# Retention of a hybrid decoder step: sample states by products of 32 rows, the head norm by ones on all partitions, and gate steps among the last head's chunks

## The chip, the cores and the metric

The kernel runs on one core of a Trainium2 chip. A core has engines with queues of their own: TensorE (PE, and PEld for loading its weights), VectorE (DVE), ScalarE (ACT), GpSimd (POOL) and SyncE (SP), which starts most transfers. The metric is the time of one execution on the device in microseconds (us); smaller is better.

## The reference

One inference step of one layer: FFN, a mixer of two branches (stick-breaking attention and retention), and another FFN. It takes a prompt of 1024 tokens and 8 decode samples of 8 tokens each. The change lies in retention (4 heads, 128 wide keys, 256 wide values) and the norm behind it:

```python
def step(S, inp):
    qi, ki, vi = inp
    inner = jnp.einsum('bhcd,bhsd->bhcs', qi, ki) * decay_in[None]
    o = jnp.einsum('bhcs,bhsv->bhcv', inner, vi) + jnp.einsum('bhcd,bhdv->bhcv', qi, S) * decay_q
    S = S * decay_c + jnp.einsum('bhsd,bhsv->bhdv', ki * decay_k, vi)
    return S, o
...
o_r, new_state = retention(q_r, k_r, v_r, ret_state)
o_rf = o_r.astype(F32)
o_rf = o_rf * lax.rsqrt(jnp.mean(o_rf * o_rf, axis=-1, keepdims=True) + NORM_EPS)
o_r = (o_rf.reshape(B, T, RET_V_WIDTH) * ret_gn_g.astype(F32)).astype(u.dtype)
o_r = jax.nn.silu(g_r) * o_r
m = jax.nn.sigmoid(a_sb) * (o_sb @ w_sb_out) + jax.nn.sigmoid(a_r) * (o_r @ w_ret_out)
```

The prompt starts from a zero state; each sample starts from its own state of 128 x 256 per head (`state_ret`), gives 8 rows of output from it and hands a new state back.

## The kernel before

Activations lie with channels on the partitions and the 1088 tokens (1024 of the prompt, 64 of the samples) along the columns. Products are in float32 precision by two means. `mm3` splits both factors into a high and a low half (`hi` on ACT, `lo` on DVE, lines 96 and 99; type fp32r) and multiplies three times (lines 133, 137, 138). A few products take plain f32 operands; the trace shows each of those as two records of MATMUL where an fp32r product is one.

`mixer_in` runs, after some of the gates: `retention()` over four heads; then 40 fill steps (`FILL_RET`); then the prompt's stick-breaking attention, 12 fill steps (`FILL_SB`) and the samples' attention over the cached pages (decode, line 1115). A fill step is three matmuls (one mm3 of one of the 8 blocks of K) of a gate projection (`gate_steps`) or of the output projection of retention (`ret_steps`); the last of a tile passes through a `gs` tile on its way to DRAM. Fill steps are also interleaved with both attentions until their supply ends, so their total is fixed. `mixer_out` follows, and begins with loads of `osT` that need the decode's last output (`odec`).

For each head, `retention()` projects q, k, v and two gates (bank `pa`), turns q and k by rope, transposes v (`ev_v`), and then goes over the prompt in four chunks of 256 tokens. A chunk makes the scores (bank `pb`), masks them (`rsc`), multiplies by v and by the state (`po`), calls `finish`, updates the state (bank `pm`), and calls `sample_states` for two of the eight samples. After the four chunks `finish` is called once more for the 64 sample tokens. So there are 16 calls of `sample_states`, and 20 of `finish`.

`sample_states` multiplies, for each sample, the 64 x 256 values under a mask (`km` x `vdn`, line 1371: the mask keeps the sample's 8 rows, a DVE operation at line 1370 and a POOL memset) and the sample's masked queries by its old state (`qm` x `s0`, line 1366, into `po_s`), and adds on DVE (line 1373). `finish` evicts the output (`oc`), squares it on ACT (439), adds (441), sums the partitions by products with one column of ones (464), forms 1/root for rows (478 on DVE, a power on POOL), makes diagonal matrices (489), and spreads them over the partitions by another product with ones (496), before DVE scales (1315) and gates (1318).

The order of instructions on each engine is set by a scheduler that simulates a timeline when the program is built; the code's order and the buffers bound it. `fill(k, after)` pins its steps behind the instruction `after`. On the chip each engine runs its list in order.

## Time and profile before

| | us |
|---|---|
| three runs | 2891.10, 2893.32, 2895.43 |
| median | 2893.32 |
| the profiled execution | 2891.72 |
| its span in the trace | 2889.2 |
| PE busy | 2798.6 (97%) |
| DVE busy | 2017.1 (70%) |
| ACT busy | 1245.3 (43%) |
| POOL busy | 738.5 (26%) |

The span is the time from the first to the last instruction that the trace holds. Times in the trace count from the span's start. Retention lies between about 820 and 1276 us, the prompt's attention behind it, decode ends at about 1940 us, and `mixer_out` begins there. PE's matmuls overlap: the time that one costs is the distance from its start to the start of the next, not its own duration. PE's granted clock is 0.99 of full speed in the mean.

### The profile page before, as it was taken

Reading aid. Unit: us, or ns where it says so; the run is one execution under the profiler, and the core shown is the slowest. Engines: PE = TensorE matmul, PEld = TensorE weight load, DVE = VectorE, ACT = ScalarE, POOL = GpSimd, SP = SyncE. Lnnn points to the kernel's source line nnn. Section 1 sums busy time; section 2 is a strip of 40 time slices with the busy share of each in tenths; the row PEclk is TensorE's granted clock in tenths of the full one; section 3 lists DMA queues with packets and bytes.
Section 4 is the critical chain, followed back from the end, with each engine's and each line's share of the span. In section 5 each row is a group of like instructions: output and inputs, shape, how many; then the busy total and the mean of one; then the engine's idle time right before and its main releaser. Section 6 shows DMA issues by size and latency. Waiting matters only on the chain.

```text
span 2889.2 us, 51617 instructions
## 1 busy us (share of the span) xinstructions
PE 2798.6 (97%) x20064; PEld 2633.3 (91%) x20064; DVE 2017.1 (70%) x3922; ACT 1245.3 (43%) x2546; POOL 738.5 (26%) x679
## 2 busy tenths in 40 slices
PE   7999999999999999999999889989999999999998
PEld 7898899999999999989999867768989988999997
DVE  7888878888753553546888744436578888688776
ACT  6444444444343333335666543213354444544443
POOL 0234513333150000000000245520013334233321
PEclk9999999999999999999999999999999999999999
DMA  6444444333252322333222389876333336333431
GB/s 177 145 127 144 140 155 123 110 112 108 80 162 83 99 84 86 94 113 80 76 74 76 123 294 332 297 244 198 105 96 121 119 110 189 122 103 107 130 89 42
DMA packets 420420, 380.63 MB, mean 132 GB/s; under 512 B 30352, under 2 KB 380944, under 8 KB 420176
## 3 DMA queue, kind: packets, MB, share of 16 engines
q1 hardware_dynamic: 397904, 306.03, 34.6%
q0 software_dynamic: 22272, 71.31, 7.4%
q8 instruction: 157, 2.57, 0.4%
q14 instruction: 87, 0.71, 0.1%
HBM read 310.03 MB, written 63.05 MB: 129 GB/s over the span
## 4 chain that ended last, share of the span: by engine, by line
PE 59%; DVE 5%; DMA 3%; issue 2%; POOL 1%; ACT 1%; SPq 0%; DVEq 0%; POOLq 0%; ACTq 0%
PE pa L133 10%; PE pa L138 10%; PE pa L137 10%; PE pb L133 3%; PE pb L138 3%; PE pb L137 3%; PE pc L137 3%; PE pc L138 3%; PE pc L133 3%; PE pc L1202 2%; PE pm L1011 1%; PE pm L1115 1%; PE pc L999 1%; DVE sl L99 1%; DMA ul<-orT 1%
## 5 line engine op out<-in xcount | busy, mean ns | idle before, releaser
L96 ACT ACTIVATE sh<-wr 128x512 fp32r<-128x512 f32 x592 | 340.0, 624 | 364.1 <-POOL wr L590 135.5
L133 PE MATMUL pa<-uh,wh 128*128 128x384 f32 (+1 forms) x1408 | 476.7, 339 | 4.2 <-ACT qdec L920 2.0
L138 PE MATMUL pa<-uh,wl 128*128 128x384 f32 (+1 forms) x1408 | 464.4, 330 | 0.0
L137 PE MATMUL pa<-ul,wh 128*128 128x384 f32 (+1 forms) x1408 | 463.5, 329 | 0.4 <-POOL ul L99 0.4
L99 DVE TENSOR_TENSOR sl<-wr,sh 128x512 fp32r<-128x512 f32 x592 | 398.8, 701 | 60.2 <-ACT sh L96 56.8
L133 PE MATMUL pa<-q,sh 128*128 128x256 f32 (+1 forms) x1408 | 410.4, 292 | 15.7 <-DVE p L648 7.8
L137 PE MATMUL pa<-q,sh 128*128 128x256 f32 (+1 forms) x1408 | 409.5, 291 | 2.2 <-DVE q L99 2.2
L138 PE MATMUL pa<-q,sl 128*128 128x256 f32 (+1 forms) x1408 | 408.5, 290 | 0.3 <-DVE sl L99 0.3
L137 PE MATMUL pc<-hl,whd 128*128 128x256 f32 (+2 forms) x1088 | 350.4, 324 | 2.6 <-DVE hl L99 2.6
L138 PE MATMUL pc<-hh,wld 128*128 128x256 f32 (+2 forms) x1088 | 350.0, 323 | 0.0
L133 PE MATMUL pc<-hh,whd 128*128 128x256 f32 (+2 forms) x1088 | 343.6, 324 | 4.5 <-DVE y L718 2.5
L718 DVE TENSOR_TENSOR y<-y,pc 128x256 f32<-128x256 f32 (+2 forms) x496 | 250.1, 516 | 135.8 <-PE pc L138 133.9
L133 PE MATMUL pb<-q,sh 128*128 128x288 f32 (+1 forms) x1088 | 314.8, 290 | 6.5 <-ACT sh L96 4.9
L138 PE MATMUL pb<-q,sl 128*128 128x288 f32 (+1 forms) x1088 | 314.6, 289 | 0.5 <-DVE sl L99 0.4
L137 PE MATMUL pb<-q,sh 128*128 128x288 f32 (+1 forms) x1088 | 314.9, 290 | 0.0
L133 PEld LDWEIGHTS pa<-q,sh 128*128 128x128 f32 x1408 | 268.2, 191 | 20.8 <-DVE p L648 8.8
L133 PEld LDWEIGHTS pa<-uh,wh 128*128 128x128 f32 x1408 | 265.7, 189 | 20.1 <-issue 10.0
L137 PEld LDWEIGHTS pa<-q,sh 128*128 128x128 f32 x1408 | 268.0, 190 | 4.7 <-DVE q L99 2.7
L137 PEld LDWEIGHTS pa<-ul,wh 128*128 128x128 f32 x1408 | 265.7, 189 | 3.3 <-issue 1.4
L138 PEld LDWEIGHTS pa<-q,sl 128*128 128x128 f32 x1408 | 267.2, 190 | 1.5 <-DVE sl L99 0.5
L138 PEld LDWEIGHTS pa<-uh,wl 128*128 128x128 f32 x1408 | 265.2, 188 | 2.7 <-issue 1.7
L588 POOL TENSOR_TENSOR wr<-wr 128x512 f32<-128x512 f32 x76 | 108.2, 1424 | 495.5 <-DVE sl L99 495.4
(340 smaller groups left out, 5958.3 us busy)
## 6 DMA issues: line engine op xcount, KB each, us to landing
wr<-in_w_ffn_gu_dram SPq DMA_DIRECT2D x176, 512.0 KB
wrd<-in_w_ffn_down_dram SPq DMA_DIRECT2D x88, 512.0 KB
wr<-in_w_in_dram SPq DMA_DIRECT2D x56, 512.0 KB
q<-cB SPq DMA_DIRECT2D x16, 576.0 KB
wr<-in_w_o_dram SPq DMA_DIRECT2D x10, 512.0 KB
cB<-y SPq DMA_DIRECT2D x32, 144.0 KB
cB<-xr SPq DMA_DIRECT2D x32, 144.0 KB
s<-in_state_ret_dram SPq DMA_DIRECT2D x16, 256.0 KB
```

The lines of the kernel that those rows point to most:

```text
L96: return self.nc.scalar.activation(dst, src, AF.Copy)
L99: (eng or self.nc.vector).tensor_tensor(dst, src, hi.bitcast(F32), op=ALU.subtract)
L133: ins = mm(ps, wh, xh, start=first, stop=False)
L137: mm(ps, wh, xl, start=False, stop=False)
L138: mm(ps, wl, xh, start=False, stop=last)
L588: tt(v1, v0, v1, op=ALU.add)
L718: nc.vector.tensor_tensor(y[p][:, d, c], y[p][:, d, c], ps[:, :n], op=ALU.add)
L999: nc.tensor.transpose(tp[:, j * P : (j + 1) * P], bt[:, j * P : (j + 1) * P], self.ident)
L1011: ins = nc.tensor.matmul(po[:, lo:256], vs[:, j, :], ats[j // 4][x][:, j % 4, lo:256], start=(j == 0 and x == 0), stop=(j == last and x == 1))
L1115: return nc.tensor.matmul(out[32 * m : 32 * m + 32], w(m), x(m), start=first, stop=last, skip_group_check=True)
L1202: ins = nc.tensor.transpose(tp[:, i * P : (i + 1) * P], kp[i // 2][:, (i % 2) * 512 + m * P : (i % 2) * 512 + (m + 1) * P], self.ident)
```

## The change

Everything is in `retention()` but for the constants and the `gs` tiles.

- **States of the samples.** A helper, `under`, lays a sample's 8 rows three times into a block of 32 rows (high, high, low of the values in `vxt`; high, low, high of the decayed keys in `kxt`; the last 8 rows are zero), so that one fp32r product of 32 rows does the work of mm3. It is called three times a head (one memset on POOL, two high parts on ACT, one low on DVE, two transposes on PE and one eviction on ACT). The products (line 1405 of the kernel after) go to the two banks `pm` and `pc`, and DVE adds twice 128 x 256 where it added once 128 x 512.
- **Outputs of the samples.** The queries (`qs`) are 8 columns, placed at column group 32*(b%4) of PE (line 1401). So `po_s` is laid out wider: the product of `sd` is made in two halves of 128 columns (1428), and four transposes of 128 x 128 at the head's end take the place of two of 64 x 64. The transposed copy of the samples' keys (`kts`) goes.
- **Head norm.** One Square of 128 x 512, an addition, a split into high and low, two fp32r products of a 128 x 128 matrix of ones (1342, 1343), then on DVE a scaling with eps and a RECIPROCAL, and on ACT a Sqrt. Row products, POOL's power, diagonals and spreading go.
- **Buffers.** `rsc` has two buffers and serves the scores, `qd` and the norm; `gs` has two where it had three.
- **Fill steps.** After each of the last head's chunks there are 8 (`FILL_CHUNK`), pinned behind the chunk's transposes of keys; `FILL_RET` is 24 where it was 40. Their total stays, so 16 leave the attentions.

The diff, cut:

```diff
+FILL_CHUNK = 8
+FILL_RET, FILL_SB = 24, 12
...
-                g = self.t(self.gstage, [P, 384], "gs", bufs=3)
+                g = self.t(self.gstage, [P, 384], "gs", bufs=2)
...
-                rq = self.t(rp, [P, RC + TD], "rq")
+                rq = self.t(rp, [P, RC + 2 * TD], "rq")
...
+                vdn = self.t(rp, [64, 256], "vdn")
+                vxt = self.t(rp, [P, 2, 256], "vxt", F32R)
+
+                def under(src, parts, dst):
+
+
+                    x = self.t(rp, [P, 256], "ux", F32R)
+                    nc.gpsimd.memset(x.bitcast(F32), 0.0)
+                    xv = x.rearrange("p (b x) -> p b x", x=32)
+                    sv = src.rearrange("p (b t) -> p b t", t=8)
+                    for i, part in enumerate(parts):
+                        if part == "h":
+                            self.hi(xv[:, :, 8 * i : 8 * i + 8], sv)
+                        else:
+                            self.lo(xv[:, :, 8 * i : 8 * i + 8], sv, xv[:, :, 0:8])
+                    pt = self.bank("pc")
+                    for g in range(2):
+                        nc.tensor.transpose(pt[:, g * P : (g + 1) * P], x.bitcast(F32)[:, g * P : (g + 1) * P],
+                                            self.ident)
+                    self.hi(dst, pt[:, :256].rearrange("p (g x) -> p g x", x=P))
...
-                    rs = self.rstd(rp, self.squares(rp, oc, n, 2, width=RC), n, 2, "pc")
+                    sq = self.t(rp, [P, 512], "rsc", bufs=2).rearrange("p (v c) -> p v c", v=2)[:, :, :n]
+                    nc.scalar.activation(sq, oc[:, :, :n], AF.Square)
+                    nc.vector.tensor_tensor(sq[:, 0], sq[:, 0], sq[:, 1], op=ALU.add)
+                    ah, al = (self.t(rp, [P, RC], x, F32R)[:, :n] for x in ("acch", "accl"))
+                    self.hi(ah, sq[:, 0])
+                    self.lo(al, sq[:, 0], ah)
+                    out = self.bank("pc")
+                    ones = self.ones.bitcast(F32R)
+                    nc.tensor.matmul(out[:, :n], ones, ah, start=True, stop=False)
+                    nc.tensor.matmul(out[:, :n], ones, al, start=False, stop=True)
+                    rs = sq[:, 1]
+                    nc.vector.tensor_scalar(rs, out[:, :n], 1.0 / (2 * P), EPS, op0=ALU.mult, op1=ALU.add)
+                    nc.vector.reciprocal(rs, rs)
+                    nc.scalar.activation(rs, rs, AF.Sqrt)
...
+                            under(vf[:, m:n], "hhl", vxt[:, :, vt * P : (vt + 1) * P])
...
-                    pS = self.bank("pm")
+                    bs = [(j, b0 + j, 32 * ((b0 + j) % 4), (b0 + j) // 4) for j in range(2)]
+                    for j, b, x, g in bs:
+                        nc.tensor.matmul(po_s[x : x + 8, g * 256 : (g + 1) * 256], qs[:, 8 * b : 8 * b + 8], s0[:, j, :],
+                                         start=False, stop=b > 3, skip_group_check=True)
+                    pS = [self.bank(t) for t in ("pm", "pc")]
+                    for j, b, x, g in bs:
+                        nc.tensor.matmul(pS[j][:, :256], kxt[x : x + 32, g, :], vxt[x : x + 32, g, :],
+                                         start=True, stop=True)
                     for j in range(2):
-                        b = b0 + j
-                        nc.tensor.matmul(po_s[:64, :256], qm[:, b * 64 : (b + 1) * 64], s0[:, j, :],
-                                         start=False, stop=b == NB - 1)
-                        km = self.t(rp, [P, P], "km", bufs=2)
-                        nc.gpsimd.memset(km[64:128, :], 0.0)
-                        nc.vector.tensor_scalar(km[:64, :], kts, ddk[:, r, b : b + 1], None, op0=ALU.mult)
-                        nc.tensor.matmul(pS[:, j * 256 : (j + 1) * 256], km, vdn, start=True, stop=True)
-                    s0f = s0.rearrange("q b v -> q (b v)")
-                    nc.vector.scalar_tensor_tensor(s0f, s0f, gam[r] ** 8, pS, op0=ALU.mult, op1=ALU.add)
+                        nc.vector.scalar_tensor_tensor(s0[:, j, :], s0[:, j, :], gam[r] ** 8, pS[j][:, :256],
+                                                       op0=ALU.mult, op1=ALU.add)
                     nc.sync.dma_start(io["ret_state_sample"][0, b0 : b0 + 2, r].rearrange("b d v -> d b v"), s0)
...
+                sd = self.t(rp, [64, 256], "sd")
+                nc.gpsimd.memset(sd, 0.0)
+                nc.vector.tensor_tensor(sd.rearrange("q (b x) -> q b x", x=32)[:, :, 0:8],
+                                        pz[:64, :64].rearrange("q (b t) -> q b t", t=8),
+                                        ddec.rearrange("q (b t) -> q b t", t=8), op=ALU.mult)
+                qs = self.t(rp, [P, TD], "qs")
+                nc.vector.tensor_tensor(qs, qf[:, TP:T], rq[:, RC : RC + TD], op=ALU.mult)
+                ks = self.t(rp, [P, TD], "ks")
+                nc.vector.tensor_tensor(ks, kf[:, TP:T], rq[:, RC + TD :], op=ALU.mult)
+                kxt = self.t(rp, [P, 2, P], "kxt", F32R)
+                under(ks, "hlh", kxt)
                 po_s = self.bank("pc")
-                nc.tensor.matmul(po_s[:64, :256], sd, vdn[:64, :], start=True, stop=False)
+                for g in range(2):
+
+                    nc.tensor.matmul(po_s[:, g * 256 : (g + 1) * 256], sd[:, g * P : (g + 1) * P], vdn,
+                                     start=g == 0, stop=False, skip_group_check=True)
...
+                        begun = nc.tensor.transpose(pt[:, s * P : (s + 1) * P],
...
+                    sc = self.t(rp, [P, 512], "rsc", bufs=2)
...
+                        qd = self.t(rp, [P, 512], "rsc", bufs=2)[:, :RC]
...
+                    if r == RH - 1:
+                        self.fill(FILL_CHUNK, begun)
...
+                for x in range(4):
+                    self.last = nc.tensor.transpose(pt[:, x * P : (x + 1) * P], on[:, x * P : (x + 1) * P],
+                                                    self.ident).ins
+                pt = pt.rearrange("q (g v b x) -> q v g b x", g=2, v=2, x=32)
+                finish([pt[:, vt, :, :, 0:8] for vt in range(2)], TP, TD)
...
```

In the pieces below, numbers behind names are those of buffers. On PE, before, in the last head's chunks (L133 to L138 are mm3):

```order
L1371 MATMUL pm_14384<-vdn_13584,km_14386 128x256
L1371 MATMUL pm_14384<-vdn_13584,km_14391 128x256
L133 MATMUL pb_14433<-rqdh_14429,rsh_14378 128x256
L137 MATMUL pb_14433<-rqdl_14430,rsh_14378 128x256
L464 MATMUL pc_14354<-ones_71,acc_14349 128x1 x2
L1409 MATMUL pc_14405<-ident_66,kf_13581 128x128
L1366 MATMUL pc_14193<-s_2619_14489,qm_14186 64x256 x2
L138 MATMUL pb_14433<-rqdh_14429,rsl_14379 128x256
L133 MATMUL pb_14433<-rsch_14423,rvh_13582 128x256
```

On PE after, in the same head; L134 to L139 are mm3, and those that write `pa` belong to fill steps:

```order
L134 MATMUL pa_14588<-uh_1743_9594,wh_14322 128x384
L138 MATMUL pa_14588<-ul_1746_9597,wh_14322 128x384
L139 MATMUL pa_14588<-uh_1743_9594,wl_14323 128x384
L1401 MATMUL pc_14223<-s_2655_14702,qs_14209 8x256
L134 MATMUL pm_14558<-rvh_13586,kdh_14491 128x256
L138 MATMUL pm_14558<-rvl_13587,kdh_14491 128x256
L1401 MATMUL pc_14223<-s_2655_14702,qs_14209 8x256
L139 MATMUL pm_14558<-rvh_13586,kdl_14492 128x256
L1342 MATMUL pc_14548<-acch_14544,ones_71 128x256
L1405 MATMUL pc_14576<-vxt_13589,kxt_14213 128x256
L1343 MATMUL pc_14548<-accl_14545,ones_71 128x256
L134 MATMUL pb_14652<-rsch_14642,rvh_13586 128x256
```

The pairs of 1371 and the two-record runs of 464 are gone; the 32-row products (1405) and the queries' (1401) stand singly among fp32r products, and the products with ones are fp32r.

On ACT before, in the last head, rows of two chunks:

```order
L1412 ACTIVATE kdh_14406<-pc_14405,rk_10390 128x128
L96 ACTIVATE rsch_14530<-rsc_14528 128x512
L1308 ACTIVATE oc_14452<-pb_14433 128x512
L96 ACTIVATE rqdh_14536<-rqd_14534 128x256
L1412 ACTIVATE kdh_14406<-pc_14405,rk_10390 128x128
L439 ACTIVATE acc_14456<-oc_14452 128x256
L439 ACTIVATE sq_14458<-oc_14452 128x256
L96 ACTIVATE rsh_14485<-rst_14483 128x256
```

On ACT after, in the same head:

```order
L1451 ACTIVATE kdh_14491<-pc_14490,rk_10390 128x128
L1326 ACTIVATE oc_14537<-pb_14518 128x512
L1347 ACT_TABLE_LOAD
L1347 ACTIVATE rsc_14413<-rsc_14413 128x256
L1335 ACTIVATE rsc_14541<-oc_14537 128x512
L1451 ACTIVATE kdh_14491<-pc_14490,rk_10390 128x128
L97 ACTIVATE acch_14544<-rsc_14541 128x256
L97 ACTIVATE rsch_14642<-rsc_14640 128x512
L805 ACT_TABLE_LOAD
L805 ACTIVATE gs_14613<-pa_14588 128x384
L1505 ACTIVATE odn_14741<-pc_14223 128x512
L97 ACTIVATE rqdh_14648<-rsc_14646 128x256
```

The square roots (1347) and the gates' sigmoids (805) now alternate, and a load of function tables stands ahead of each; there are 16 such loads in the program that were not there, 2 in each of the first three heads and 10 in the last.

On SP before, where the decode ends and `mixer_out` begins (`odec` is the decode's output; `sq` are mixer_out's loads of it):

```order
L874 DMA mrT_84<-gs_22239 128x384
L146 DMA wr_22958<-in_w_o_dram 128x8x128
L1275 DMA osT_79<-odec_19195 128x4x64
L1528 DMA sq_22306<-osT_79 128x512
L874 DMA mrT_84<-gs_22268 128x320
L1528 DMA sq_22310<-osT_79 128x512
```

On SP after, at the same place:

```order
L147 DMA wr_22932<-in_w_o_dram 128x8x128
L1570 DMA sq_22312<-osT_79 128x512
L1570 DMA sq_22316<-osT_79 128x512
L875 DMA mrT_84<-gs_22274 128x320
L1276 DMA osT_79<-odec_19263 128x4x64
L1570 DMA sq_22320<-osT_79 128x512
L1570 DMA sq_22324<-osT_79 128x512
```

Two of the `sq` loads (of the columns that are the prompt's alone) now stand ahead of the store of `odec`, and a load of `w_o` behind it.

## Rows read from the trace of the kernel before

**Rows 1.** Busy time by stretch: us, then busy and count of each engine.

```profile
core 0: us, PE busy (x) PEld busy (x) DVE busy (x) ACT busy (x) POOL busy (x), PEclk, DMA share, GB/s
900.00:1000.00 100.00, 100.00 (x634) 94.81 (x633) 50.38 (x120) 35.13 (x79) 6.17 (x15) 1.00 0.30 92
...
1249.00:1276.00 27.00, 24.61 (x170) 20.92 (x169) 21.66 (x58) 13.01 (x32) 3.75 (x9) 1.00 0.38 115
```

**Rows 2.** PE's waits, 865 to 1300 us: line, releaser, total, times, longest.

```profile
PE pc L1366 <- DMA s<-in_state_ret_dram: 1.2, 1, 1.2
PE pc L464 <- DVE acc L441: 0.6, 1, 0.6
PE pb L137 <- DVE rscl L99: 0.3, 1, 0.3
PE pm L133 <- ACT kdh L1412: 0.3, 1, 0.3
```

**Rows 3.** Timeline of PE, last head: start, duration, line, tile, columns, records.

```profile
1255.06 1.02 PE L1371 MATMUL pm<-vdn,km 128*128 128x256 f32 x4
...
1256.04 0.28 PE L138 MATMUL pb<-rsch,rvl 128*128 128x256 f32 x1
1256.16 0.28 PE L133 MATMUL pb<-rsch,rvh 128*128 128x256 f32 x1
```

**Rows 4.** The same timeline, a run of the samples' queries.

```profile
1252.04 0.28 PE L138 MATMUL pb<-rqh,rkhl 128*128 128x256 f32 x1
1252.26 1.08 PE L1366 MATMUL pc<-s,qm 128*64 128x256 f32 x4
...
1253.48 0.28 PE L137 MATMUL pm<-rvl,kdh 128*128 128x256 f32 x1
```

**Rows 5.** The same timeline, products of the head norm and a transpose.

```profile
1253.72 0.50 PE L464 MATMUL pc<-ones,acc 128*128 128x1 f32 x4
1254.08 0.30 PE L1409 MATMUL pc<-ident,kf 128*128 128x128 f32 x1
...
1254.34 0.28 PE L133 MATMUL pb<-rqh,rkh 128*128 128x256 f32 x1
...
1256.75 0.27 PE L1409 MATMUL pc<-ident,kf 128*128 128x128 f32 x1
...
1256.98 0.28 PE L133 MATMUL pb<-rsch,rvh 128*128 128x256 f32 x1
...
1258.64 0.61 PE L496 MATMUL pc<-ndg,ones 128*128 128x128 f32 x4
...
1259.21 0.28 PE L133 MATMUL pb<-rsch,rvh 128*128 128x256 f32 x1
```

**Rows 6.** Timeline of PE, second head: the samples' products with 64 rows.

```profile
927.88 0.27 PE L1386 MATMUL pc<-ident,kf 128*64 128x128 f32 x1
928.09 0.64 PE L1390 MATMUL pc<-vdn,sd 64*64 64x256 f32 x2
928.66 0.33 PE L1409 MATMUL pc<-ident,kf 128*128 128x128 f32 x1
```

**Rows 7.** Timeline of PE in decode: four products side by side.

```profile
1801.18 0.43 PE L1115 MATMUL pm<-vpage,at 128*32 128x128 f32 x8
1801.54 0.44 PE L133 MATMUL pa<-uh,wh 128*128 128x384 f32 x1
```

**Rows 8.** Timeline of ACT in the first FFN: a load of function tables.

```profile
32.97 0.63 ACT L96 ACTIVATE sh<-wr 128x512 fp32r<-128x512 f32 x1 [7.30 <-DMA wr<-in_w_ffn_gu_dram]
33.61 1.28 ACT L626 ACT_TABLE_LOAD   x1
34.91 0.38 ACT L626 ACTIVATE hf<-pa 128x256 f32<-128x256 f32 x1
```

**Rows 9.** Groups of DVE, 820 to 1300 us: busy us, mean ns, idle before.

```profile
L441 DVE TENSOR_TENSOR acc<-acc,sq 128x256 f32<-128x256 f32 x16 | 6.7, 417 | 0.0
L1373 DVE SCALAR_TENSOR_TENSOR s<-s,pm 128x512 f32<-128x512 f32 x16 | 10.9, 680 | 1.4 <-PE pm L1371 1.2
L1370 DVE TENSOR_SCALAR km<-odn,ddk 64x128 f32<-64x128 f32 x32 | 8.7, 283 | 0.2
```

**Rows 10.** PE's waits, 1900 to 1960 us.

```profile
PE pa L133 <- ACT sh L96: 7.6, 1, 7.6
```

More of the change, by code (lines that the diff above doesn't have):

```diff
@@ L41 @@
 GATES_FIRST = 4
-FILL_RET, FILL_SB = 40, 12
+FILL_CHUNK = 8
+FILL_RET, FILL_SB = 24, 12
 FILL_HEADS = ((2, 4), (2, 4), (2, 4), (2, 2))
@@ L802, in gate_steps @@
                     if k == KD - 1:
-                        g = self.t(self.gstage, [P, 384], "gs", bufs=3)
+                        g = self.t(self.gstage, [P, 384], "gs", bufs=2)
                         nc.scalar.activation(g[:, :n], ps[:, :n], AF.Sigmoid)
@@ L870, in ret_steps @@
                 if k == KD - 1:
-                    g = self.t(self.gstage, [P, 384], "gs", bufs=3)
+                    g = self.t(self.gstage, [P, 384], "gs", bufs=2)
                     nc.sync.dma_start(g[:, :n], self.gbT[d * P : (d + 1) * P, o : o + n])
@@ L1288, in retention @@
             nc.sync.dma_start(rk, io["c_rk"])
-            ddk = self.t(rp, [64, RH, NB], "ddk")
-            nc.sync.dma_start(ddk, io["c_ddk"])
             for r in range(RH):
@@ L1301, in retention @@
                 vl = self.t(rp, [P, 8, 256], "rvl", F32R)
-                vdn = self.t(rp, [P, 256], "vdn")
-                nc.gpsimd.memset(vdn[64:128, :], 0.0)
+                vdn = self.t(rp, [64, 256], "vdn")
[15 more added lines that the diff above has]
+                    self.hi(dst, pt[:, :256].rearrange("p (g x) -> p g x", x=P))
                 def finish(src, o, n):
                     oc = self.t(rp, [P, 2, RC], "oc", bufs=2)
-                    nc.scalar.activation(oc[:, :, :n], src, AF.Copy)
+                    if n == RC:
+                        nc.scalar.activation(oc[:, :, :n], src, AF.Copy)
+                    else:
+                        for vt in range(2):
+                            nc.scalar.activation(oc[:, vt, :n].rearrange("q (g b x) -> q g b x", g=2, x=8), src[vt],
+                                                 AF.Copy)
                     gs = self.t(rp, [P, 2, RC], "rgs", bufs=1)
@@ L1347, in ev @@
                         if m < n:
-                            nc.scalar.activation(vdn[:64, vt * P : (vt + 1) * P], pt[:64, 256:384], AF.Copy)
+                            nc.scalar.activation(vdn[:, vt * P : (vt + 1) * P], pt[:64, 256:384], AF.Copy)
+                            under(vf[:, m:n], "hhl", vxt[:, :, vt * P : (vt + 1) * P])
                     return ev
@@ L1408, in retention @@
                     for s in range(2):
-                        nc.tensor.transpose(pt[:, s * P : (s + 1) * P],
-                                            kf[:, m * RC + s * P : m * RC + (s + 1) * P], self.ident)
+                        begun = nc.tensor.transpose(pt[:, s * P : (s + 1) * P],
+                                                    kf[:, m * RC + s * P : m * RC + (s + 1) * P], self.ident).ins
                         dk = rk[:, r, s : s + 1]
@@ L1461, in retention @@
                     sample_states(2 * m)
-                on = self.t(rp, [64, 256], "odn")
-                nc.scalar.activation(on, po_s[:64, :256], AF.Copy)
+                    if r == RH - 1:
+                        self.fill(FILL_CHUNK, begun)
+                on = self.t(rp, [P, 512], "odn")
+                nc.scalar.activation(on, po_s, AF.Copy)
                 pt = self.bank("pc")
-                for vt in range(2):
-                    self.last = nc.tensor.transpose(pt[:, vt * 64 : (vt + 1) * 64], on[:, vt * P : (vt + 1) * P],
-                                                    self.ident[:64, :64]).ins
-                finish(pt[:, :128].rearrange("q (v c) -> q v c", v=2), TP, TD)
+                for x in range(4):
[3 more added lines that the diff above has]
+                finish([pt[:, vt, :, :, 0:8] for vt in range(2)], TP, TD)
     def mixer_in(self, ends, done):
@@ L1792, in _constants @@
     b = np.arange(TD) // 8
-    out["c_rq"] = np.concatenate([np.exp(lg[:, None] * (c + 1.0)), np.exp(lg[:, None] * (t + 1.0))], 1).astype(f)
+    out["c_rq"] = np.concatenate([np.exp(lg[:, None] * (c + 1.0)), np.exp(lg[:, None] * (t + 1.0)),
+                                  np.exp(lg[:, None] * (7.0 - t)) * sc], 1).astype(f)
     df = t[None, :] - t[:, None]
@@ L1797, in _constants @@
                      * sc).astype(f)
-    out["c_ddk"] = (np.exp(lg[None, :, None] * (7.0 - t)[:, None, None])
-                    * (b[:, None] == np.arange(NB)[None, :])[:, None, :] * sc).astype(f)
     return {k: np.ascontiguousarray(v) for k, v in out.items()}
```

13 lines of the change are left out of this document (removed).

## Prediction

> **What bounds the kernel now.** First the busy time by stretch. In retention's heads PE is busy without a gap (100.00 of 100 us), DVE half of the time and ACT a third; the granted clock is 1.00 [rows 1]. Only the last head's chunks, 1249 to 1276 us, show PE idle: 24.61 busy of 27, so 2.39 idle, with DVE at 21.66 and ACT at 13.01 [rows 1]. The list of PE's waits says the same: over all of retention four waits and 2.4 us, the longest 1.2 for a load of a sample's state [rows 2]. So in three heads of four the end is set by PE's own work. A saving on DVE or POOL is worth nothing there; a saving on PE is worth its full time as long as nothing else comes to be late. The prices of PE's work come from its timeline, as distances between starts [rows 3 to 7].
>
> **What PE sheds.** The step of an fp32r product with 256 columns is 0.12 us [rows 3]. Two plain f32 products of 256 columns (1371) take 1256.04 - 1255.06 = 0.98 with the one step behind them, so 0.86, or 0.43 each [rows 3]; 32 go: 13.8 us. Two of 1366, with as many columns but a tile of 128 x 64, take 1253.48 - 1252.04 = 1.44 less two steps, 1.20 [rows 4]. That is 0.34 more than 1371's pair, and I put it down to entering and leaving the narrow tile, once for each run. There are 32 such products in 20 runs: 13.8 + 6.8 = 20.6 us. Of the head norm, the row sums take 1254.34 - 1253.72 = 0.62 less a step and a transpose (0.23 less a step, 0.11), 0.39; the spreading takes 0.57 less a step, 0.45 [rows 5]. Twenty finishes at 0.84 make 16.8; I take the four short ones at the same price. The transpose of the samples' keys (0.21) and the `sd` product (0.57) take 0.78 a head, 3.1 together [rows 6]. The eight small transposes at the heads' ends, at 0.11 to 0.21 by the two transposes of [rows 5, 6], taken near the upper: 1.5. Sum shed: 13.8 + 20.6 + 16.8 + 3.1 + 1.5 = 55.8 us.
>
> **What PE takes on.** The norm's 40 fp32r products: 40 x 0.12 = 4.8. Forty transposes (24 in `under`, 16 at the ends): 40 x 0.11 = 4.4. The 8 halves of `sd`, which stand singly: a 64-row product costs between 0.57 [rows 6] and 0.43 + 0.34 = 0.77; at 0.77, 6.2. The queries (1401): 32 products in 19 runs, 13 of them pairs. The two of a pair lie in different column groups, and decode shows that such products run together: four of 128 columns take 0.36 to the next start [rows 7], where in sequence they would take four times half of 0.43, 0.86. So I price a pair as one, 19 x 0.77 = 14.6; in sequence it would be 13 x 1.20 + 6 x 0.77 = 20.2. The 32-row products (1405): 32, nearly all single among fp32r products. No row shows a 32-row tile. Low end 0.12 each, 3.8 in all; high end 0.12 + 0.34 = 0.46 each, 14.7, if a short tile costs what a narrow one does. I take the high end: it is nearest to the run of 1366 [rows 4]. Sum taken on: 4.8 + 4.4 + 6.2 + 14.6 + 14.7 = 44.7. **PE's net: 11.1 us less**; bounds 5.5 (queries in sequence) and 22.0 (row tiles free).
>
> The row for this is the 0.34 of a narrow run [rows 4]. The Trainium skill, TensorEngine Tiling (Array Packing), section Key Properties, says that a change of the tiling mode drains the TensorE; it speaks against the 32-row products standing singly, and no run here shows such a tile yet.
>
> **The last head.** Its 2.4 us of idle time [rows 1, 2] should go, since 32 fill steps now stand there, and those need nothing from the chunks. What is new is ACT's work: ten loads of tables (the order shows a sigmoid or a root behind each), at 34.91 - 33.61 = 1.30 each [rows 8] 13.0 us on top of ACT's 13.01, where PE's work goes from 24.6 to some 38 (a quarter of 11.1 less, and 32 fill steps of three matmuls of about 0.17, 16.6). ACT's list runs in order: while it stands at a root that waits for DVE's RECIPROCAL, the sigmoid that frees a `pa` bank and the high parts for the next chunk queue behind it, and PE waits for those. DVE stays near 24: it loses the masks (8 x 0.283) and the diagonals, and gains in each of four finishes a split, a scaling and a RECIPROCAL (0.417 each if they cost what another operation of 256 columns does [rows 9]). Each engine has room, but they take turns. I put new waits at 3 us, with 0 and 10 as bounds: 10 is three quarters of the loads' time. Net of the last head: 0.6 lost. In the first three heads there are six loads, and ACT is idle for two thirds [rows 1]: nothing.
>
> ACT's row shows the next activation 1.30 us after the load's start [rows 8]. The Trainium skill, ScalarE: Activation LUTs, section What ACT_TABLE_LOAD costs, gives 1283 ns for the load, as the trace has it, and a drain of 1380 ns more; by 2.66 us a switch, ten would hold ACT for 26.6 us in the last head, and the time would go to that of the third rival. The row leaves no place for the drain.
>
> **The rest.** POOL loses its powers and masks; nothing waits for it. Sixteen fill steps (8 us of PE) leave the attentions for retention: work moved, not shed. But about ten fewer stand behind the last decode product, and `mixer_out` begins with a wait of 7.6 us for a split of `osT` [rows 10]. With less work to lie under it the wait can grow by up to 5; with two of the four loads now ahead of the store of `odec` on SP it can shrink, by about half at most, 4. I take 0. With two `gs` buffers a load runs less far ahead of its use; SP's list waits in order for the stores in front, so 0 to 2 us; I take 0.
>
> **Sum.** Against the profiled execution, 2891.72 - 11.1 + 0.6 = 2881.2. The median of the runs is 1.6 above that execution, so **2882.8**.
>
> **Rivals.** About 0.2% (5.8 us) is what a measurement of this kernel can tell from no change.
>
> *Row tiles are free.* The 32-row products fit among the others at 0.12: 10.9 less, 2872. For it: with so few rows they might begin before the product ahead has drained; against: the narrow tile's 0.34.
>
> *Queries in sequence.* Both products of a pair go to the same bank and use different operands; if they follow each other, 5.6 is lost, 2888.4: no change. Against it: decode's products, which write one bank together [rows 7].
>
> *The last head turns on ACT and DVE.* If the RECIPROCAL takes not one but eight times an addition's time, four of them in the last head bring DVE up to PE there: at 8 x 0.42 = 3.3 each, 11.6 us more than reckoned, DVE at 36 against 38 of PE with the chain in turns, and the waits go to 10: 2889.8, no change. The row is only that of an addition. The Trainium skill, VectorE: DVE Perf Modes, in its walkthrough of the 8-slice pipeline, says that Reciprocal divides iteratively with a repeat count of 8; no run here shows one yet, and the factor of 8 is an estimate from that page.
>
> *Slower: every finish holds PE.* Square, addition, split, ones, scaling, RECIPROCAL and root are one chain through ACT, PE, DVE and ACT again, and on ACT the next chunk's high parts queue behind the root. If this chain costs PE more than 0.85 us in each of 20 finishes, 17 us, the 11 are eaten and 6 more: 2899 and above. Against it: in three heads projections and gates of the next head lie between, and ACT and DVE are half idle [rows 1].
>
> **How the numbers follow.** Forecast 0.50 (own range 2877 to 2888.5), row tiles free 0.17, in sequence 0.11, the last head 0.13, slower 0.09. Faster by over 0.2% (under 2887.5): the first two and a few parts of the third, less the forecast's upper edge: 0.70. Within: 0.21. Slower: 0.09. The range is 2869 to 2892: it leaves out the slower rival and the tails of the free tiles and of the last head.
>
> **What would show it.** In the trace of the kernel after: the step from a 32-row product's neighbour to the next (0.46 more or 0.12 more than without); a pair of 1401 at 0.77 or 1.20; two products of ones at 0.24; PE still busy to 100 in the first heads; PE's idle time from the last head's begin to the end of its fill at 3 us or less, and none of it put down to `gs` or to the root; the RECIPROCAL at about 0.42; the wait at the begin of `mixer_out` near 7.6. The prediction is wrong if PE's waits in the first three heads add up to more than 2 us, or if a 32-row or 8-column product costs more than 1 us.

## The result, and the profile after

The change makes the kernel slower. The median of nine runs is 2900.9 us (2898.6 to 2901.5), that of the kernel before in the same nine rounds 2893.3; the ratio is 1.0025 with a 95% interval of 1.0015 to 1.0034. The profiled execution took 2900.28 us, its span is 2898.5. The forecast was 2882.8 in a range of 2869 to 2892.

I cut both traces into stages, at PE's first and last instruction of retention, decode's first and last product, and the first product of `mixer_out`. In each stage I counted the products of 384 and 320 columns (fill steps and projections) at their 0.1735 and 0.147 us, and PE's idle time; what is left is "rest": the work that the change touches, beside attention and decode's own.

| stage | before: length | fill | idle | rest | after: length | fill | idle | rest |
|---|---|---|---|---|---|---|---|---|
| ahead of retention | 897.9 | | | | 900.6 | | | |
| retention | 381.7 | 255.3 | 2.4 | 124.0 | 396.3 | 273.0 | 7.6 | 115.8 |
| to decode's first product | 378.7 | 247.3 | 11.3 | 120.2 | 377.6 | 238.0 | 20.5 | 119.1 |
| decode | 272.5 | 104.1 | 9.2 | 159.3 | 270.2 | 100.8 | 12.4 | 157.0 |
| to mixer_out | 17.1 | 8.7 | 7.6 | 0.7 | 9.2 | 3.7 | 4.6 | 0.9 |
| mixer_out to the end | 933.4 | | | | 937.4 | | | |

Fill is the same in sum, 615.4. The rest shrinks by 8.3 + 1.1 + 2.2 - 0.2 = 11.4. The first two, 9.4, are the change's: 1.1 in the second stage, since the last products of the old norm stood there. The 2.2 of decode are not, for nothing in it was touched, and its rest is anything from 153.5 to 160.0 among the profiles of this study. So most of the work is gone, as forecast. But PE's idle time grows by 5.2 + 9.2 + 3.2 - 3.0 = 14.6, and the stage behind by 4.0. (The stage ahead of retention holds nothing of the change; it varies from 896 to 904 among the profiles of this study.)

The largest piece is one wait. PE's waits around decode's begin, after (line, releaser, total, times, longest):

```profile
PE pc L1116 <- ACT qd L1134: 11.1, 1, 11.1
PE pc L1000 <- DVE pt L1048: 3.3, 2, 2.0
PE pc L1203 <- ACT kt L1210: 1.9, 1, 1.9
```

and the first of these before:

```profile
PE pc L1115 <- POOL qd L1106: 3.1, 1, 3.1
```

ACT's timeline there, after (start, duration, line, what; in brackets its idle time and what ended it):

```profile
1660.96 0.49 ACT L805 ACTIVATE gs<-pa 128x384 f32<-128x384 f32 x1 [3.39 <-PE pa L139]
1662.66 0.60 ACT L1210 ACTIVATE kt<-pc 128x512 f32<-128x512 f32 x1 [1.21 <-PE pc L1203]
1667.58 0.94 ACT L97 ACTIVATE uh<-ul 128x384 fp32r<-128x384 f32 x2 [4.32 <-DMA ul<-orT]
1670.55 1.99 ACT L97 ACTIVATE uh<-ul 128x384 fp32r<-128x384 f32 x4 [2.03 <-DMA ul<-orT]
1672.92 0.94 ACT L97 ACTIVATE uh<-ul 128x384 fp32r<-128x384 f32 x2 [0.37 <-DMA ul<-orT]
1673.76 0.69 ACT L1134 ACTIVATE qd<-qdec 64x32 f32<-64x32 f32 x4
```

And before:

```profile
1654.54 0.60 ACT L1209 ACTIVATE kt<-pc 128x512 f32<-128x512 f32 x1 [1.21 <-PE pc L1202]
1657.61 0.70 ACT L1133 ACTIVATE qd<-qdec 64x32 f32<-64x32 f32 x4 [2.47 <-POOL qd L1106]
...
1675.80 1.95 ACT L96 ACTIVATE uh<-ul 128x384 fp32r<-128x384 f32 x4 [2.90 <-DMA ul<-orT]
```

`ul` is retention's output, loaded back from DRAM and split (`ret_prep`) for the last kind of fill step, the output projection. Before, its first splits stood 18 us behind the copies of decode's first queries (`qd`). After, they stand ahead of them: ACT waits 6.7 us for three loads, splits, and only then copies the queries, for which PE has waited since 1663.4. The supply of fill steps is one list; whoever takes 16 steps more ahead of the attention comes 16 steps earlier to what stands behind them in the list, and that was a load with a split.

In retention, PE's busy time by stretch (the answer to [rows 1]; the last head's chunks now reach to 1291):

```profile
900.00:1000.00 100.00, 100.00 (x628) 93.58 (x627) 52.07 (x107) 41.95 (x91) 1.25 (x4) 1.00 0.27 82
1249.00:1276.00 27.00, 21.56 (x131) 18.18 (x130) 16.62 (x33) 12.62 (x23) 0.00 (x0) 0.94 0.38 117
```

and PE's waits (the answer to [rows 2]):

```profile
PE pb L134 <- ACT rsch L97: 3.4, 1, 3.4
PE pc L1448 <- DVE kdl L1452: 2.0, 3, 1.0
PE pa L134 <- ACT rxs L1372: 1.6, 3, 0.6
```

The last head was to lose its waits under 32 fill steps, and has more: in the same 27 us PE is busy for 21.56 where it was for 24.61, at a granted clock of 0.94 where it was 1.00.

### The profile page after: what moved, and what is told of

Same layout as the page of the kernel before. It is cut to its first block, busy times and chain, and to the rows that moved or that the text cites. A ratio compares the mean times of both kernels' runs of the same rounds, so it can differ in the third digit from the quotient of the medians.

```text
span 2898.5 us, 51386 instructions
## 1 busy us (share of the span) xinstructions
PE 2791.9 (96%) x19964; PEld 2621.4 (90%) x19964; DVE 2043.8 (71%) x3926; ACT 1285.0 (44%) x2618; POOL 720.0 (25%) x635
## 4 chain that ended last, share of the span: by engine, by line
PE 79%; DVE 10%; issue 4%; DMA 3%; POOL 2%; ACT 1%; SPq 0%; DVEq 0%; POOLq 0%; ACTq 0%
PE pa L134 13%; PE pa L138 12%; PE pa L139 12%; PE pb L134 5%; PE pb L138 5%; PE pb L139 5%; PE pc L138 5%; PE pc L139 5%; PE pc L134 5%; PE pc L1203 2%; DVE sl L100 2%; DMA ul<-orT 1%; DVE pt L1050 1%; PE pm L1116 1%; PE pb L1116 1%
## 5 line engine op out<-in xcount | busy, mean ns | idle before, releaser
L134 PE MATMUL pa<-uh,wh 128*128 128x384 f32 (+1 forms) x1408 | 476.5, 339 | 5.2 <-ACT rxs L1372 1.6
L139 PE MATMUL pa<-uh,wl 128*128 128x384 f32 (+1 forms) x1408 | 464.8, 330 | 0.0
L138 PE MATMUL pa<-ul,wh 128*128 128x384 f32 (+1 forms) x1408 | 464.2, 330 | 0.4 <-POOL ul L100 0.4
L134 PE MATMUL pa<-q,sh 128*128 128x256 f32 (+1 forms) x1408 | 410.1, 291 | 14.9 <-DVE p L649 7.8
L138 PE MATMUL pa<-q,sh 128*128 128x256 f32 (+1 forms) x1408 | 409.7, 291 | 2.2 <-DVE q L100 2.2
L139 PE MATMUL pa<-q,sl 128*128 128x256 f32 (+1 forms) x1408 | 408.5, 290 | 0.3 <-DVE sl L100 0.3
L138 PE MATMUL pc<-hl,whd 128*128 128x256 f32 (+2 forms) x1088 | 350.5, 324 | 2.6 <-DVE hl L100 2.6
L139 PE MATMUL pc<-hh,wld 128*128 128x256 f32 (+2 forms) x1088 | 350.0, 323 | 0.0
L134 PE MATMUL pc<-hh,whd 128*128 128x256 f32 (+2 forms) x1088 | 343.6, 324 | 4.7 <-DVE y L719 2.6
L134 PE MATMUL pb<-q,sh 128*128 128x288 f32 (+1 forms) x1088 | 315.0, 290 | 7.1 <-ACT sh L97 5.5
L139 PE MATMUL pb<-q,sl 128*128 128x288 f32 (+1 forms) x1088 | 314.5, 289 | 0.5 <-DVE sl L100 0.4
L138 PE MATMUL pb<-q,sh 128*128 128x288 f32 (+1 forms) x1088 | 314.8, 290 | 0.0
L134 PEld LDWEIGHTS pa<-uh,wh 128*128 128x128 f32 x1408 | 266.1, 189 | 22.6 <-issue 11.3
L134 PEld LDWEIGHTS pa<-q,sh 128*128 128x128 f32 x1408 | 268.0, 190 | 19.6 <-DVE p L649 8.8
L138 PEld LDWEIGHTS pa<-q,sh 128*128 128x128 f32 x1408 | 267.9, 190 | 4.7 <-DVE q L100 2.7
L138 PEld LDWEIGHTS pa<-ul,wh 128*128 128x128 f32 x1408 | 266.2, 189 | 4.3 <-issue 1.9
L139 PEld LDWEIGHTS pa<-q,sl 128*128 128x128 f32 x1408 | 267.3, 190 | 1.5 <-DVE sl L100 0.5
L139 PEld LDWEIGHTS pa<-uh,wl 128*128 128x128 f32 x1408 | 265.8, 189 | 2.3 <-issue 1.2
L589 POOL TENSOR_TENSOR wr<-wr 128x512 f32<-128x512 f32 x76 | 108.6, 1428 | 495.6 <-DVE sl L100 491.9
```

The source lines that it names most:

```text
L134: ins = mm(ps, wh, xh, start=first, stop=False)
L138: mm(ps, wh, xl, start=False, stop=False)
L139: mm(ps, wl, xh, start=False, stop=last)
L589: tt(v1, v0, v1, op=ALU.add)
```

## The experiments

Runs of different groups were made on different chips, on which the kernel before itself had medians from 2891 to 2900; so each is compared by its ratio to the kernel before in the same rounds. Theory A: the moved fill steps lose the time, through the splits ahead of decode's queries. Rival B: the new norm loses it, in retention.

**The fill steps put back, and moved alone.**

```diff
-FILL_CHUNK = 8
-FILL_RET, FILL_SB = 24, 12
+FILL_CHUNK = 0
+FILL_RET, FILL_SB = 40, 12
```

> The kernel after with the fill steps where they were (none among the last head's chunks, 40 behind retention). Theory A: the 16 steps that moved bring the splits of retention's output (uh from ul) ahead of decode's first queries (qd) on ACT, and PE waits 11.1 us there where it waited 3.1; here the queries stand first again, the wait is 3 to 4 us, what hangs on it in decode and at mixer_out goes too, and the time is 2888 to 2893. Rival B: the time is lost in retention, to the root's table loads and the RECIPROCAL on the in-order lists of ACT and DVE (PE idle 7.6 us there against 2.4); then the time stays at 2897 to 2901.

Measured: ratio 0.9999 (0.9990 to 1.0008). The second kernel is the one before with `FILL_CHUNK = 8` and `FILL_RET = 24`:

> The kernel before with the fill steps of the change alone (8 after each chunk of the last head, 24 behind retention), old states and old norm. Theory A: PE waits about 11 us for decode's first queries, and the time is 2899 to 2905. Rival B: nothing is lost, the last head's 2.4 us of waits are covered, 2890 to 2893.

Measured: 1.0030 (1.0019 to 1.0040). PE's wait for the queries, with the fill put back:

```profile
PE pc L1116 <- POOL qd L1107: 2.3, 1, 2.3
```

and with the fill moved alone:

```profile
PE pc L1116 <- ACT qd L1134: 11.2, 1, 11.2
```

So the moved steps cost the kernel before about as much (0.30%) as they cost the kernel after (1.0025 beside 0.9999), and bring the whole loss: theory A. The run with the fill moved alone shows each piece of the table again: PE idles 20.5 us ahead of decode, 12.0 in decode and 4.5 ahead of `mixer_out`, and the stage behind takes 938.3. Rival B falls as the cause of the loss. It keeps a share: with the fill put back the shed work brings nothing (0.9999), for PE idles 10.1 us in retention, and at a granted clock of 0.98 in that stage its rest shrinks by 3.7 alone, to 120.3. The fill alone does cover the last head's old waits: 0.2 us of idle time are left in retention.

**The same number ahead of the attention, in the new place.**

```diff
-FILL_RET, FILL_SB = 24, 12
+FILL_RET, FILL_SB = 8, 12
```

> The kernel after with 8 fill steps behind retention in place of 24: with the 32 among the last head's chunks that makes 40 ahead of the attention, as many as before. Theory A (it is the count ahead of the attention that puts the splits of retention's output before decode's first queries, and not their place among the chunks): the wait for the queries is 2 to 4 us as before, the last head keeps its cover and a higher clock than with no fill there, and the time is 2884 to 2889. Rival C (fill steps among the chunks cost by themselves): 2893 or more.

Measured: 0.9983 (0.9972 to 0.9994), slightly faster than the kernel before. No wait for `qd` is left among PE's waits at decode's begin, though the 32 steps still lie among the chunks. It is the count ahead of the attention that decides, not the place. Its retention stage is that of the kernel after to 0.1 us (7.6 idle, 115.7 rest).

**The order of queries and splits.** Two attempts keep the 56 steps ahead of the attention (32 among the chunks, 24 behind retention). One moves the copies of the queries to DVE (`nc.vector.tensor_copy` for `nc.scalar.activation`):

> The kernel after with the copies of decode's queries (qd) on DVE, so that they no longer queue behind the splits on ACT. Theory A: the 11.1 us wait falls to 3 to 5 us and the time to 2890 to 2895, unless the eviction kt behind the same splits waits in its place, then 2896 to 2900. Rival B: 2900 to 2902.

Measured: 1.0032 (1.0022 to 1.0042), and PE still waits 10.8 us, now for DVE: the low halves of the same splits stand ahead of the queries there too. The other adds one order on ACT:

```diff
-                self.hi(h[:, k, :n], lf[:, k, :n])
+                split = self.hi(h[:, k, :n], lf[:, k, :n])
+                if self.query is not None:
+                    self.behind(split, self.query)
```

> The kernel after, with one order added: on ACT the splits of retention's output (uh from ul) stand behind the copies of decode's first queries (qd). The number of fill steps ahead of the attention is that of the kernel after. Theory A: the wait of 11.1 us for the queries falls to about 3. If it was the queries alone that were late, the time falls by 8, a ratio of 0.9995 to 1.000 to the kernel before. If the evictions kt, which now stand behind the splits and their loads, are late in place of the queries, PE waits 5 to 8 us for those and the ratio stays at 1.0015 to 1.003.

Measured: 1.0006 (0.9996 to 1.0016). PE's wait for the queries is gone; two others stand in its place:

```profile
PE pc L1182 <- DVE bt L1160: 6.0, 1, 6.0
PE pc L1205 <- DVE kt L1210: 5.5, 1, 5.5
```

ACT in that run shows why: the splits with their loads now stand between the queries and the next eviction.

```profile
1668.50 0.69 ACT L1136 ACTIVATE qd<-qdec 64x32 f32<-64x32 f32 x4
1672.04 0.94 ACT L97 ACTIVATE uh<-ul 128x384 fp32r<-128x384 f32 x2 [2.85 <-DMA ul<-orT]
1673.58 0.94 ACT L97 ACTIVATE uh<-ul 128x384 fp32r<-128x384 f32 x2 [0.60 <-DMA ul<-orT]
1675.86 1.88 ACT L97 ACTIVATE uh<-ul 128x384 fp32r<-128x384 f32 x4 [1.34 <-DMA ul<-orT]
1677.64 0.58 ACT L1212 ACTIVATE kt<-pc 128x512 f32<-128x512 f32 x1
```

By the ratios about three quarters of the 0.25% went with the order, but that share isn't shown: the intervals of the two ratios touch, and the profile has no such gain. Between retention and `mixer_out` PE idles 34.8 us in it, where the kernel after has 37.5, and from retention's start to PE's last instruction it takes 1994.6 us for 1990.7 (the profiled execution was 3.5 us above this kernel's median). What the run does show is that the same loads and splits hold up whatever stands behind them.

**Norm and states, each alone,** with the fill of the kernel before:

> The kernel before with the head norm by ones alone (RECIPROCAL and Sqrt, two buffers of rsc and of gs), old states, fill steps in their old places. PE sheds 20 x 0.84 - 4.8 = 12 us. If the root's table loads and the RECIPROCAL make the last head's waits, PE idles 6 to 10 us in retention and the time is 2886 to 2891; if they come from the states' new form, PE idles 2 to 3 us there and the time is 2880 to 2884.

Measured: 0.9988 (0.9977 to 0.9999); PE idles 10.1 us in retention and its rest there is 118.9.

> The kernel before with the samples' states by 32-row products alone (queries in 8 columns, wider po_s), old head norm, fill steps in their old places. By the prices measured in the kernel after (0.51 for a 32-row product, 0.73 for a run of queries, 0.78 for a half of sd, 0.11 a transpose) PE takes on 40.8 us and sheds 39: 2892 to 2896. If the waits of the last head come from the states' new form, 2896 to 2900.

Measured: 0.9994 (0.9982 to 1.0006); 3.4 us idle, rest 124.0, as before. So the states' new form is worth nothing on PE and costs 1 us of waits; what PE sheds, it sheds by the norm, and most of the last head's waits come with the norm too. In the run with the norm alone the granted clock is 0.76 between 1260 and 1270 us, where PE was busy for 5.93 of 10, so part of its work ran at the lower level of the clock on top of the waits.

**RECIPROCAL or tables.** Three kernels with 8 steps behind retention. The first has one function of ACT for 1/root:

```diff
-                    nc.vector.reciprocal(rs, rs)
-                    nc.scalar.activation(rs, rs, AF.Sqrt)
+                    nc.scalar.activation(rs, rs, AF.Abs_reciprocal_sqrt)
```

> As the run with 8 fill steps behind retention, with 1/root as one function of ACT (Abs_reciprocal_sqrt) in place of RECIPROCAL on DVE and Sqrt on ACT; the table loads stay. If the RECIPROCAL (1.75 us, 20 times) makes the last head's waits, PE's 7.6 us of idle time in retention fall to 2 to 4 and the ratio from 0.9983 to 0.997; if the table loads make them, 6 to 9 us and 0.998 to 0.999.

Measured: 0.9974 (0.9963 to 0.9985), the lowest ratio of this study, and faster than the kernel before; its interval overlaps that of the run with 8 steps alone (0.9983), so it isn't shown to beat that one. PE idles 5.0 us in retention; the waits for `rxs` in the first heads and for `kdl` in the last are gone, those for `rsch` stay at 3.7. Its rest in retention is 121.5, though, 5.8 more than with 8 steps alone: between 1260 and 1280 us its granted clock is 0.70 and 0.66. The profiled execution, 2891.2, is 4.7 us above this kernel's median, so the trace doesn't show where the ratio comes from; the shorter decode in it (267.3 for 271.9) is nothing that the edit touches.

> As the run with 8 fill steps behind retention, without the Sqrt (the norm's factor is then 1/variance), so without its table loads; the RECIPROCAL stays. One look at the trace: if the table loads make the waits, PE idles 2 to 4 us in retention; if the RECIPROCAL makes them, 6 to 8.

Measured in one execution: 2884.8 us, beside a median of 2894.1 of the kernel before; 6.0 us idle, at a granted clock of 1.00 all through retention; `rxs` 1.6 and `kdl` 1.8 stay, `rsch` falls from 3.4 to 1.9.

> As the run with 8 fill steps behind retention, without the RECIPROCAL (the norm multiplies by the root); Sqrt and its table loads stay. One look at the trace: if the table loads make the waits, PE idles 6 to 8 us in retention; if the RECIPROCAL makes them, 2 to 4.

Measured in one execution: 2885.4 us; 4.6 us idle, with the waits of the run with one function. So both have a share. The RECIPROCAL makes the 2.0 for `kdl`, which stands behind it in DVE's list of the kernel after:

```profile
1256.94 1.75 DVE L1346 RECIPROCAL rsc<-rsc 128x256 f32<-128x256 f32 x1
1258.61 0.25 DVE L1452 SCALAR_TENSOR_TENSOR kdl<-pc,rk,kdh 128x128 fp32r<-128x128 f32 x1
```

The 1.6 for `rxs` goes with it, but isn't shown to be its doing: the run with pairs and the old norm, below, has no RECIPROCAL and waits 1.7 us for `rxs`. The tables make about half of the 3.4, ACT's list holding `rsch` behind them. Neither run comes to the 2 to 4 us that a single cause would have left.

The root by a power on POOL, which would have had neither, was a mistake of price:

> The kernel after with the head norm's root as one power of 128 x 256 on POOL in place of RECIPROCAL and Sqrt: no table loads. Theory A: retention wins up to 5 us of idle time, the wait for decode's first queries stays at about 11: 2895 to 2899. Rival B: all of the loss was there, 2888 to 2892. If the power on POOL is slow (over 2 us for 256 columns) the chunks wait for it instead: 2900 to 2906.

Measured: 1.143 (1.142 to 1.145). The trace has the reason, 41 us for one power of 256 columns:

```profile
L1346 POOL TENSOR_TENSOR rsc<-rsc,mhalf 128x256 f32<-128x256 f32 x16 | 657.5, 41117 | 34.5 <-DVE rsc L1345 34.5
```

**The 32-row products in pairs.** They are kept together by a priority and an order:

```diff
+                    head = state(*bs[0])
+                    with self.tc.high_priority():
+                        self.behind(state(*bs[1]), head.ins)
```

> As the run with 8 fill steps behind retention, and the two 32-row products of a call are kept next to each other on PE (16 pairs in place of 32 single ones). Where two stood next to each other by chance their starts were 0.01 us apart. If a pair costs what a single one does (0.51), PE sheds 8 us more: 2877 to 2882. If the second waits for the first, the cost is in the entering and leaving alone: 4 to 5 us less, 2880 to 2885. If keeping them together holds PE back (two banks must be free at once): 2885 to 2892.

Measured: 0.9992 (0.9981 to 1.0003). The two start within 0.01 us of each other. But PE then waits:

```profile
1004.75 0.28 PE L139 MATMUL pb<-rqh,rkhl 128*128 128x256 f32 x1
1004.96 0.38 PE L1405 MATMUL pm<-vxt,kxt 32*128 32x256 f32 x1
1004.96 0.38 PE L1405 MATMUL pc<-vxt,kxt 32*128 32x256 f32 x1
1005.27 0.66 PE L1512 MATMUL pc<-ident,odn 128*128 128x128 f32 x4
1008.86 0.42 PE L1342 MATMUL pc<-acch,ones 128*128 128x64 f32 x1 [2.93 <-ACT acch L97]
```

In the new order the samples' norm (1342) stands right behind the last pair and the transposes that its squares come from, with nothing between; in each of the first three heads that is 2.93 us, and 13.4 us of idle time in retention. I tried to take this wait away twice. Writing the samples' end behind the next head's projections:

> As the run with the states in pairs (8 fill steps behind retention), and in the first three heads the samples' last transposes and norm are written behind the next head's projections, so that PE has other work while the chain Square, addition, split runs. The three waits of 2.9 us for the high part of the squares (8.8 us in all) go: 8 us less than with pairs alone, a ratio of 0.996 to 0.997.

Measured: 0.9994 (0.9984 to 1.0003), with the same three waits: the scheduler put the instructions where it had put them before. And the old norm where the new one waits:

> States in pairs, 8 fill steps behind retention, and the norm by ones only where ACT and DVE are half idle (the four chunks of the first three heads); the last head and the samples' tokens keep the old norm. Against the run with pairs and the norm by ones throughout: the three waits of 2.9 us for the samples' squares and the last head's waits for root and RECIPROCAL go (13.4 us of idle time in retention fall to 2 to 4), PE takes on 8 x 0.6 = 5 us of old norms. Ratio to the kernel before 0.995 to 0.9965. If the waits belong to the new states and not to the norm, idle time stays over 8 us and the ratio is 0.998 or more.

Measured: 1.0005 (0.9993 to 1.0016), 10.3 us idle, 7.8 of it for the samples' squares in the old norm too. So this wait belongs to the order, not to the norm; the next run, with pairs and the old norm, has another order and none of it. The old norm throughout, with pairs and the 40 steps:

> States by 32-row products in pairs, old head norm, 8 fill steps after each of the last head's chunks and 8 behind retention. PE sheds 8 us by the pairs against the states alone (which were worth nothing), and the last head's waits are covered, without tables and RECIPROCAL: 9 to 11 us less than the kernel before, a ratio of 0.9962 to 0.997. If the norm by ones is worth more than its waits, the run with the late norm beats this one.

Measured: 0.9985 (0.9975 to 0.9996); rest 118.9 in retention, 4.0 idle. That is 5 us less rest than with the states alone, where I expected 8, and some 4 us less time than the kernel before, where I expected 9 to 11. A pair does take what one product takes (0.51, below). Between fill steps of 0.1735 us it costs 955.83 - 954.97 = 0.86 less two steps, 0.51:

```profile
954.97 0.34 PE L138 MATMUL pa<-ul,wh 128*128 128x384 f32 x1
955.23 0.38 PE L1392 MATMUL pm<-vxt,kxt 32*128 32x256 f32 x1
955.24 0.38 PE L1392 MATMUL pc<-vxt,kxt 32*128 32x256 f32 x1
955.55 0.44 PE L139 MATMUL pa<-uh,wl 128*128 128x384 f32 x1
955.83 0.28 PE L134 MATMUL pb<-rqdh,rsh 128*128 128x256 f32 x1
```

And the fill moved with 40 in sum, everything else old:

> The kernel before with 8 fill steps after each of the last head's chunks and 8 behind retention (40 ahead of the attention, as before), old states, old norm. PE's 2.4 us of waits in the last head go and nothing else moves: 2 to 3 us less, a ratio of 0.9985 to 0.9995. It also tells what norm and states are worth with the same fill: the run of the kernel after with 8 behind retention had 0.9983.

Measured: 1.0007 (0.9997 to 1.0017). In retention only 0.2 us of idle time are left, as expected, but 3.7 us of new waits come at decode's begin and 2.0 at the attention's; the gain is given back. Beside the 0.9983 of the kernel after with the same fill, norm and states together are worth some 0.24%, 7 us, though on different chips.

## Why the prediction was wrong

**What PE sheds: about right.** Forecast 11.1 us, measured 9.4 by the table (8.3 in retention and 1.1 behind it). Some of the 8.3 hides the lower clock: in the run without the Sqrt, whose products are the same, the clock is 1.00 and retention's rest 114.4, so 9.6 less. The prices of the new products, from PE's timeline after:

```profile
1004.75 0.34 PE L134 MATMUL pa<-uh,wh 128*128 128x384 f32 x1
1005.01 0.38 PE L1405 MATMUL pm<-vxt,kxt 32*128 32x256 f32 x1
1005.33 0.44 PE L138 MATMUL pa<-ul,wh 128*128 128x384 f32 x1
1005.61 0.34 PE L139 MATMUL pa<-uh,wl 128*128 128x384 f32 x1
...
1246.71 0.28 PE L139 MATMUL pm<-rvh,kdl 128*128 128x256 f32 x1
1246.92 0.60 PE L1401 MATMUL pc<-s,qs 128*8 128x256 f32 x4
1247.46 0.44 PE L134 MATMUL pa<-uh,wh 128*128 128x384 f32 x1
1247.74 0.33 PE L138 MATMUL pa<-ul,wh 128*128 128x384 f32 x1
```

A 32-row product costs 1005.61 - 1004.75 less two steps of 0.1735, so 0.51; I had taken 0.46, my upper end, from a narrow tile [rows 4]. A pair of queries costs 1247.74 - 1246.71 less 0.12 and 0.1735, so 0.74; I had 0.77. With these two prices my sum would have been 10.1. The Trainium skill, TensorEngine Tiling (Array Packing), section Key Properties, says that a change of the tiling mode drains the engine and that different tiles can run in parallel; the 0.39 above a plain step of 0.12, and the pairs that take what one takes, agree with both. The rivals of free row tiles and of queries in sequence both fall.

**The last head: right in direction, too small.** I forecast new waits of 3 us in place of 2.4; PE idles 7.6 us in retention, and 1.6 of it in the first three heads, where I had nothing. The term that was mis-sized is that of the new waits, and within it the RECIPROCAL, which I priced like an addition [rows 9]:

```profile
L1346 DVE RECIPROCAL rsc<-rsc 128x256 f32<-128x256 f32 x16 | 28.0, 1748 | 0.2
L1345 DVE TENSOR_SCALAR rsc<-pc 128x256 f32<-128x256 f32 x16 | 6.7, 420 | 1.0 <-PE pc L1343 0.8
```

It takes 1.75 us, 4.2 times its neighbour. The Trainium skill, VectorE: DVE Perf Modes, in its walkthrough of the 8-slice pipeline, has a repeat count of 8 for it; I carried that as a rival with 3.3 us, an estimate, and the measured 1.75 lies between that and the addition's 0.42. The tables were priced right: 1.28 us each, the next activation 1.30 us after the load's start. The Trainium skill, ScalarE: Activation LUTs, section What ACT_TABLE_LOAD costs, adds a drain of some 1380 ns; again this trace has no room for it.

```profile
1265.00 1.05 ACT L97 ACTIVATE wh<-wr 128x1024 fp32r<-128x1024 f32 x1
1266.06 1.28 ACT L805 ACT_TABLE_LOAD   x1
1267.36 0.44 ACT L805 ACTIVATE gs<-pa 128x320 f32<-128x320 f32 x1
1267.69 0.62 ACT L1335 ACTIVATE rsc<-oc 128x512 f32<-128x512 f32 x1
1268.21 0.62 ACT L97 ACTIVATE rsch<-rsc 128x512 fp32r<-128x512 f32 x1
```

This is the 3.4 us wait for `rsch`: a gate's weights, a table, the gate and a Square stand ahead of the chunk's scores on ACT. The 5.2 us more of idle time alone would have left the time in the forecast's range; the run with 8 steps behind retention, 0.9983 or some 2888 us, is that case, with about half of the forecast gain.

**"Sixteen fill steps ... work moved, not shed": this step failed.** In the part on the rest I put their move at nothing. I looked at where they leave (decode's end) and at where they arrive, but not at what moves up behind them. The list of fill steps ends in steps with loads and splits of their own, and moving sixteen brought the first of these from behind decode's first queries to ahead of them. That is 8 us at the queries (11.1 for 3.1) and 1.2 elsewhere ahead of decode, another 3.2 in decode, less 3.0 at `mixer_out`, whose wait did not grow but shrank (4.6 for 7.6; I had allowed 5 more or 4 less, and taken 0). Whether the 3.2 in decode come from the splits, or from decode having some six fill steps fewer to cover its waits (100.8 us of fill for 104.1), no run separates. What came on top lies behind. With the same 6474 instructions on PE, `mixer_out` to the end took 4.0 us longer, all of it in the first forty products (15.7 us for 11.6): 1.6 of it is a longer wait for DVE's `xr` (1.9 for 0.3), and with the rest the granted clock is lower. The stretches there, after:

```profile
1955.00:1960.00 5.00, 4.70 (x14) 3.65 (x14) 2.29 (x4) 1.26 (x2) 0.00 (x0) 0.62 1.04 386
1960.00:1965.00 5.00, 3.07 (x14) 2.22 (x13) 2.68 (x6) 1.63 (x4) 0.00 (x0) 1.00 1.12 343
1965.00:1970.00 5.00, 5.00 (x17) 3.90 (x16) 3.42 (x7) 2.72 (x6) 0.00 (x0) 0.66 0.97 315
```

The granted clock is 0.62 and 0.66 there, between the levels of 1.2 and 2.4 GHz, and in the stretch between PE idles 1.9 us; before, the stretches behind the wait had 0.86 and 1.00. This goes with the moved steps: the stage takes 935.8 to 938.3 in the five profiles with 56 steps ahead of the attention, and 932.0 to 935.9 in the thirteen with 40. Why the clock came back later after a shorter wait, no run here settles.

**The rival that ends on the other side: wrong place.** I had the finishes' chain hold PE in every head, 17 us in all, for 2899 and above. The measured 2900.9 lies there by chance: PE's waits in the first three heads are 1.6 us in all. No rival had a fill step's load, and neither of my two signs that the prediction is wrong (over 2 us of waits in the first three heads, a product over 1 us) would have found the fault.

## What to carry to other kernels

When work is taken from a shared supply to cover a hole, list what comes earlier by that on every engine, loads and splits behind the moved steps above all, and look where these now stand in the in-order lists; hold the number of steps ahead of the next stage constant, and change only their place (here, with norm and states old, that measured 1.0007, with 1 inside its interval). Price an operation by a row of itself: an addition is no stand-in for RECIPROCAL, and a power of a few columns none for one of 256. Where PE sheds work in a stage with waits on two other engines, count what those engines must do instead, for the stage may hand the gain back, in waits and, as in some of these runs, in the clock.

## What the runs showed of the hardware that I had not expected

Two 32-row products on different row groups, side by side, take 0.51 us together, what one takes alone. A power on POOL takes 41 us for 128 x 256, some 0.16 us a column; the norm before asked it for 2 columns at a time, at 0.77 us each, and none of PE's waits in retention was put down to it. A RECIPROCAL of 128 x 256 on DVE takes 1.75 us, and one function of ACT (Abs_reciprocal_sqrt, 0.38 us in the mean) takes the place of it and of Sqrt.
